# Six orders of the matmuls in the block pairs of two feed-forwards

## Chip, cores and metric

The kernel runs on one core of one Trainium2 chip. The metric is the device time of one execution in microseconds (us); for several executions the median is taken. One core has TensorE (matmuls), VectorE (DVE in the rows), ScalarE (ACT), GpSimd (POOL) and SyncE (SP), each with its own instruction queue, and 16 DMA engines that all queues share. Matmuls write into PSUM, which has eight banks; all else lies in SBUF.

## What is computed

One layer of a streaming encoder for 512 new frames of one stream and 64 of another, together 576 columns, with 1024 features on the rows. Cut to what matters here:

```python
x = x + 0.5 * swiglu_ffn(rms_norm(x, ffn1_norm), ffn1_w_gate_up, ffn1_w_down)   # 1024 -> 2 x 2816 -> 1024
...                                                   # mixer: products by w_in, two convolutions,
...                                                   # w_a_out, w_b_out, w_out
x = x + 0.5 * swiglu_ffn(rms_norm(x, ffn2_norm), ffn2_w_gate_up, ffn2_w_down)

def swiglu_ffn(x, w_gate_up, w_down):
    gate, up = jnp.split(x @ w_gate_up, 2, axis=-1)
    return (jax.nn.silu(gate) * up) @ w_down
```

All values are fp32. The hidden width is 2816, that is 22 tiles of 128, numbered i = 0 to 21.

## The kernel before

**Products in three parts.** Each fp32 operand is split into a high part that TensorE takes in one pass and a low part, the rest. A product is then three matmuls for each 128 x 128 piece of weights: high weights by high activations, high by low, low by high. The stationary operand is always a 128 x 128 piece of weights, the moving one half of the frames, 288 columns. In a plain product (`mm`, lines 431 to 442) both halves of the frames are done piece by piece into two banks, in the order of `SIX`: four matmuls on the high weights, alternating between the halves, then two on the low ones.

**Block pairs.** For most tiles i the gate and the up projection are not made by four plain products but by seven block products on sums and differences (a scheme of seven products for a 2 x 2 block matrix). `pair(i, hs, last)` (lines 863 to 907) does one tile: for n = 0 to 6 it fetches unit n of the weights with `ws.get`, calls `block` with that unit and operand list `bs[n]`, and runs `steps[n - 1]`, which reads finished banks with ScalarE or VectorE. Of the moving operands, n = 0, 2, 3 and 4 are the first half of their tiles, n = 1, 5 and 6 the second. `block` (lines 452 to 459) takes one bank and writes its twelve matmuls k by k (four pieces of 128 rows), each time high-high, high-low, low-high. Feed-forward 1 has 18 such pairs (i = 4 to 21), feed-forward 2 has 21 (i = 1 to 21), in four groups of 5, 5, 6 and 6 tiles; after each group come the products by `w_down` for it. Pairs are 39 x 84 = 3276 of the 9718 matmul instructions.

**Weights.** `Stream` (lines 202 to 318) loads raw weights by SyncE's queue, and makes from each a unit: ScalarE casts the high part; the low part is made by VectorE (`how` "dve"), or ScalarE writes minus the high part and a DMA of GpSimd's queue adds the raw weights to it ("dma"). In a pair units 0, 4 and 6 are "dma", the others "dve". `ws.get(n)` begins units up to six ahead, so where it stands in the program sets where these casts and subtractions stand in the queues of ScalarE and VectorE. Each engine works its queue in program order. Units live in turn in four tiles `u` (high and low part in one tile) and in tiles `g` (one for each part).

**Left over from a pair.** The last steps of a pair (the second half of up, the hidden product, its split) go into `rest`, and the next pair pops one after each block. In feed-forward 2 tile 0 is a plain one whose gate, hidden product and split also wait in `rest` for pair 1.

**Sums over partitions** (`Sum.total`, lines 592 to 614) are four matmuls with a matrix of ones, `ones_r`, between products.

Of the kernel before, what the change touches and what calls it, by code (L numbers as in the profile page):

```python
# [22 lines left out]
KU = KT // 2  # L23
T = SEQ + DSEQ
H = T // 2
# [86 lines left out]
def tile_encoder_step(  # L112
# [51 lines left out]
    def bank():  # L164

        if not spare:
            t = psum2()
            spare.extend((t[:, 0, :], t[:, 1, :]))
        return spare.pop(0)
# [279 lines left out]
            got += [(w, kk) for kk in range(ws.units[n][1])]  # L449
        return got  # L450

    def block(w, xs):

        q = bank()[:, :H]
        for k in range(KU):
            (whi, wlo), (xh, xl) = w, xs[k]
            for m, (l, r) in enumerate(((whi, xh), (whi, xl), (wlo, xh))):
                pe.matmul(q, l[:, k, :], r, start=k == m == 0, stop=k == KU - 1 and m == 2)
        return q


# [358 lines left out]
    def ffn(f, xg, sums, finish, forms, R=None, todo=()):  # L820
        todo = list(todo)

        rest = []


        def plain(i, hs):
            nonlocal R
            t, up = ttile(), (f, "u", i)
            ps = product((f, "g", i), xg, order=IN_TURN if f == "f2" and i == 0 else None)
            got = None if up in early else chunks(up)  # L830
            if R is None:
                R = rstd(sums)
            ups = product(up, xg, got=got)
            hs.append(None)
            at = len(hs) - 1

            def gate():
                dve.tensor_tensor(halves(t), ps, halves(R), op=ALU.mult)
                sca.activation(t, t, AF.Silu)

            def hidden():
                dve.tensor_tensor(halves(t), ups, halves(t), op=ALU.mult)
                hs[at] = high(t)

            def parts():
                hs[at] = hs[at], low(t, hs[at])

            if f == "f2":
                rest.extend((gate, hidden, parts))
                return  # L850
            gate()
            forming()
            hidden()
            forming()
            parts()
            forming()

        def forming():
            if todo:
                for step, p in todo.pop(0):  # L860
                    step(p)

        def pair(i, hs, last):
            qu, uu, t, cu = (ttile() for _ in range(4))
            q1, u2, u3, u4 = half(qu, 0), half(qu, 1), half(uu, 0), half(uu, 1)
            q = []

            def q7():
                dve.tensor_tensor(u3, q[3], u2, op=ALU.add)
                dve.tensor_tensor(half(cu, 1), u3, q[2], op=ALU.subtract)  # L870

            def gate():
                dve.tensor_tensor(half(t, 1), q[5], u4, op=ALU.add)
                dve.tensor_tensor(t, t, R, op=ALU.mult)
                sca.activation(t, t, AF.Silu)

            steps = (
                lambda: sca.copy(q1, q[0]),
                lambda: dve.tensor_tensor(u2, q[1], q1, op=ALU.subtract),
                lambda: dve.tensor_tensor(u4, q[2], u2, op=ALU.subtract),  # L880
                q7,
                lambda: dve.tensor_tensor(half(t, 0), q[4], q1, op=ALU.add),
                gate,
            )
            for n, xs in enumerate(bs):
                q.append(block(ws.get(plan[f, "s", i][n]), xs))
                if n > 0:
                    steps[n - 1]()
                if rest:
                    rest.pop(0)()  # L890

            hs.append(None)
            at = len(hs) - 1

            def up():
                if last:
                    dve.tensor_tensor(t, t, R, op=ALU.mult)
                dve.tensor_tensor(half(cu, 0), q[6], u3, op=ALU.add)

            def hidden():  # L900
                dve.tensor_tensor(cu, cu, t, op=ALU.mult)
                hs[at] = high(cu)

            def parts():
                hs[at] = hs[at], low(cu, hs[at])

            rest.extend((up, hidden, parts))

        for g, grp in enumerate(GROUPS):
            hs = []  # L910
            for i in grp:
                if i < PLAIN[f]:
                    plain(i, hs)
                    continue
                if i == PLAIN[f]:
                    ws.ahead = AHEAD_UNITS
                    bs = forms.operands(xg)
                pair(i, hs, grp[-1] == FT - 1)
            while rest:
                rest.pop(0)()  # L920
            spare.clear()
            if grp[-1] < FT - 1:
                for j, ps in enumerate(both([(f, "d", g, j) for j in range(2)], hs, turn=True)):
                    update(j, ps, R)
                for j in range(2, KT):
                    update(j, product((f, "d", g, j), hs), R)
            else:
                finish(g, hs)
# [509 lines left out]
```

## Time and profile before

| what | value |
|---|---|
| median of three runs | 1294.17 us (1290.7 to 1296.05) |
| span of the profiled execution, first to last instruction | 1290.1 us |
| TensorE busy | 1279.4 us, 99% |
| VectorE, ScalarE, GpSimd busy | 925.1, 765.5, 361.6 us |
| mean granted TensorE clock | 0.997 of full speed |

The profile is of one execution; its own time outside the trace is not given apart from the three runs, so its span stands beside their median. A row of the timeline begins with the start in us from the span's beginning and a length in us, then engine, line, operation, the tiles out<-in, the shapes and how many equal instructions in a row (x12) it stands for. Nearly every instruction is issued through one helper, line 88, so the tile names tell them apart. Lengths of matmuls overlap, since they are pipelined: the pace is read from the starts of successive rows, divided by the count.

### The profile page before, as it was taken

The numbers are of one execution on the slowest core, as the hardware profiler recorded it, in microseconds if no ns is written. First come the engines' busy times: TensorE is split into PE (matmuls) and PEld (weight loads), VectorE is DVE, ScalarE is ACT, GpSimd is POOL, SyncE is SP. The second block draws the span as 40 slices with busy tenths as digits, with TensorE's granted clock in tenths as the row PEclk, the third lists the DMA queues.
The fourth block names the chain that finished last, engine by engine and source line by source line (L and its number), as shares of the span: only waits on it lengthen the run. The fifth ranks groups of instructions, "written<-read, shape, count | busy, mean of one in ns | idle before, by whom it ended". The sixth has DMA issues, their size and how long they took to land.

```text
span 1290.1 us, 25702 instructions
## 1 busy us (share of the span) xinstructions
PE 1279.4 (99%) x9728; PEld 1277.5 (99%) x9728; DVE 925.1 (72%) x1539; ACT 765.5 (59%) x1359; POOL 361.6 (28%) x460
## 2 busy tenths in 40 slices
PE   9999999999999999999999999999999999999997
PEld 9999999999999999999999999999999999999997
DVE  6868668748846998888895166656867848847956
ACT  7655646646776645555444576477665655654664
POOL 0032332232333444333321221122142141241230
PEclk9999999999999999999999999999999999999998
DMA  7286787886799898788885767696687696796783
GB/s 220 70 181 154 163 180 155 177 181 149 154 224 232 174 200 173 165 172 174 172 172 124 163 142 154 151 236 145 139 175 171 151 197 151 164 204 138 158 172 97
DMA packets 286812, 215.26 MB, mean 167 GB/s; under 512 B 15456, under 2 KB 248928, under 8 KB 286688
## 3 DMA queue, kind: packets, MB, share of 16 engines
q0 software_dynamic: 56160, 92.43, 43.3%
q1 hardware_dynamic: 228784, 120.35, 32.8%
q8 instruction: 77, 1.26, 0.4%
q10 hardware_dynamic: 1744, 0.83, 0.2%
q14 instruction: 47, 0.39, 0.1%
HBM read 116.17 MB, written 4.98 MB: 94 GB/s over the span
## 4 chain that ended last, share of the span: by engine, by line
PE 92%; issue 4%; DVE 2%; DMA 1%; ACT 1%; POOL 0%; DVEq 0%; POOLq 0%; ACTq 0%
PE mm L88 92%; DVE tmp L88 0%; DMA g<-raw 0%; DMA raw<-in_w_b_out_dram 0%; DVE x L88 0%; DVE g L88 0%; DMA u<-raw 0%; ACT act L88 0%; DVE w L88 0%; POOL u L88 0%; DVE act L88 0%; ACT u L88 0%; ACT w L88 0%; ACT g L88 0%; POOL g L88 0%
## 5 line engine op out<-in xcount | busy, mean ns | idle before, releaser
L88 PE MATMUL mm<-act,u 128*128 128x288 f32 x4758 | 668.3, 293 | 0.1
L88 PEld LDWEIGHTS mm<-act,u 128*128 128x128 f32 x4758 | 638.9, 188 | 0.4 <-DMA u<-raw 0.3
L88 PE MATMUL mm<-act,g 128*128 128x288 f32 x3030 | 432.9, 294 | 0.9 <-DMA g<-raw 0.9
L88 PEld LDWEIGHTS mm<-act,g 128*128 128x128 f32 x3030 | 410.3, 188 | 1.1 <-DMA g<-raw 1.1
L88 POOL DMA_DIRECT2D u<-raw x197 | 172.3, 874 | 481.7 <-ACT u L88 317.4
L88 PE MATMUL mm<-act,act 128*128 128x288 f32 (+2 forms) x1896 | 259.9, 293 | 0.0
L88 PEld LDWEIGHTS mm<-act,act 128*128 128x128 f32 x1896 | 252.2, 188 | 0.5 <-ACT act L88 0.3
L88 ACT CAST u<-raw 128x512 fp32r<-128x512 f32 (+2 forms) x207 | 118.8, 574 | 172.0 <-PE mm L88 136.7
L88 POOL DMA_DIRECT2D g<-raw x126 | 109.9, 872 | 297.4 <-ACT g L88 242.7
L88 DVE SCALAR_TENSOR_TENSOR w<-g,prm,w 128x606 f32<-128x606 f32 x232 | 179.3, 844 | 1.4 <-ACT w L88 1.4
L88 DVE TENSOR_TENSOR tmp<-mm,tmp 128x288 f32<-128x288 f32 (+1 forms) x251 | 112.9, 459 | 70.3 <-PE mm L88 53.7
L88 ACT ACTIVATE u<-u 128x512 fp32r<-128x512 f32 (+2 forms) x197 | 116.8, 593 | 6.2
L88 ACT CAST g<-raw 128x512 fp32r<-128x512 f32 (+2 forms) x136 | 75.1, 553 | 43.9 <-DMA raw<-in_ffn_w_down_dram 17.6
L88 DVE SCALAR_TENSOR_TENSOR tmp<-mm,r 128x576 f32<-128x576 f32 x48 | 36.3, 757 | 76.6 <-PE mm L88 76.6
L88 POOL DMA_DIRECT2D act<-raw x67 | 59.1, 883 | 108.3 <-ACT act L88 94.5
L88 ACT CAST act<-tmp 128x576 fp32r<-128x576 f32 x92 | 61.9, 675 | 43.1 <-DVE tmp L88 42.1
L88 ACT CAST g<-w 128x512 fp32r<-128x512 f32 x79 | 49.0, 620 | 64.4 <-DVE w L88 58.6
L88 ACT CAST u<-w 128x512 fp32r<-128x512 f32 x81 | 50.2, 619 | 61.0 <-DVE w L88 43.6
L88 DVE TENSOR_TENSOR act<-tmp,act 128x576 fp32r<-128x576 f32 x92 | 67.5, 754 | 18.1 <-ACT act L88 16.5
L88 ACT ACTIVATE g<-g 128x512 fp32r<-128x512 f32 (+2 forms) x126 | 72.1, 572 | 4.0
L88 DVE TENSOR_TENSOR w<-raw,raw 128x512 f32<-128x512 f32 x82 | 56.2, 685 | 16.2 <-DMA raw<-in_ffn_w_gate_up_dram 11.2
L88 ACT ACTIVATE tmp<-tmp 128x576 f32<-128x576 f32 x47 | 32.2, 686 | 45.1 <-DVE tmp L88 45.0
(86 smaller groups left out, 830.6 us busy)
## 6 DMA issues: line engine op xcount, KB each, us to landing
raw<-in_ffn_w_gate_up_dram SPq DMA_DIRECT2D x171, 256.0 KB, 3.5
u<-raw POOLq DMA_DIRECT2D x140, 256.0 KB, 4.2
raw<-in_w_in_dram SPq DMA_DIRECT2D x112, 256.0 KB, 3.8
raw<-in_ffn_w_down_dram SPq DMA_DIRECT2D x96, 192.0 KB, 3.8
g<-raw POOLq DMA_DIRECT2D x69, 256.0 KB, 4.2
act<-raw POOLq DMA_DIRECT2D x61, 256.0 KB, 4.4
g<-raw POOLq DMA_DIRECT2D x43, 192.0 KB, 4.5
u<-raw POOLq DMA_DIRECT2D x41, 192.0 KB, 4.5
```

Of the source, the lines that this page charges most:

```text
L88: return self.tc.keep_in_program_order(fn(*args, **kwargs))
```

## The change

`block` gets a parameter v that picks one of six orders for the three kinds of matmul (HH high-high, HL high weights by low activations, LH low weights by high activations); `blocks` writes them and sets start and stop by the first and last matmul of each product. The pair of tile i uses v = i mod 6. Order 0 is that of before. Order 2 does two pieces' high matmuls and then their two low ones, order 3 swaps HH and HL, order 4 does all high matmuls and then the four low ones, order 5 begins each piece with LH. With v = 1, blocks 0 and 1, 2 and 3, 4 and 5 are written side by side into two banks, by `TURNS`; both units are fetched, and both blocks issued, before the step that followed the first one. Block 6 of such a pair has order 0. The mixer's two block pairs call `block` without v.

```diff
-    def block(w, xs):
-
-        q = bank()[:, :H]
-        for k in range(KU):
-            (whi, wlo), (xh, xl) = w, xs[k]
-            for m, (l, r) in enumerate(((whi, xh), (whi, xl), (wlo, xh))):
-                pe.matmul(q, l[:, k, :], r, start=k == m == 0, stop=k == KU - 1 and m == 2)
+    HH, HL, LH = range(3)
+
+    BLOCK_ORDERS = (
+        [(k, m) for k in range(KU) for m in (HH, HL, LH)],
+        None,
+        [(k + d, m) for k in (0, 2) for d, m in (
+            (0, HH), (0, HL), (1, HH), (1, HL), (0, LH), (1, LH))],
+        [(k, m) for k in range(KU) for m in (HL, HH, LH)],
+        [(k, m) for k in range(KU) for m in (HH, HL)] + [(k, LH) for k in range(KU)],
+        [(k, m) for k in range(KU) for m in (LH, HH, HL)],
+    )
+
+    def blocks(parts, orders):
+
+        qs = [bank()[:, :H] for _ in parts]
+        for n, (i, k, m) in enumerate(orders):
+            (whi, wlo), xs = parts[i]
+            xh, xl = xs[k]
+            l, r = ((whi, xh), (whi, xl), (wlo, xh))[m]
+            mine = [o for o in orders if o[0] == i]
+            pe.matmul(
+                qs[i], l[:, k, :], r, start=(i, k, m) == mine[0], stop=(i, k, m) == mine[-1]
+            )
+        return qs
+
+    TURNS = [
+        (i, k, m) for k in range(KU)
+        for i, m in ((0, HH), (0, HL), (1, HH), (1, HL), (0, LH), (1, LH))
+    ]
+
+    def block(w, xs, v=0):
+
+        q, = blocks([(w, xs)], [(0, k, m) for k, m in BLOCK_ORDERS[v]])
         return q
...
+            v = i % len(BLOCK_ORDERS)
             for n, xs in enumerate(bs):
-                q.append(block(ws.get(plan[f, "s", i][n]), xs))
+                if v == 1 and n < 6:
+                    if n % 2 == 0:
+                        two = [(ws.get(plan[f, "s", i][n + d]), bs[n + d]) for d in range(2)]
+                        q.extend(blocks(two, TURNS))
+                else:
+                    q.append(block(ws.get(plan[f, "s", i][n]), xs, 0 if v == 1 else v))
                 if n > 0:
                     steps[n - 1]()
```

**TensorE, pair 1 of feed-forward 2, before**, from the middle of block 0 into block 1. The names are the PSUM tile, the moving tile, and the stationary one: `g_11152` and `g_11153` are the high and low part of unit 0, `u_11181` holds both parts of unit 1.

```order
6030 L88 MATMUL mm_11390<-act_10968,g_11152 128x288
6031 L88 MATMUL mm_11390<-act_10969,g_11152 128x288
6032 L88 MATMUL mm_11390<-act_10968,g_11153 128x288
6033 L88 MATMUL mm_11390<-act_11128,g_11152 128x288
6034 L88 MATMUL mm_11390<-act_11129,g_11152 128x288
6035 L88 MATMUL mm_11390<-act_11128,g_11153 128x288
6036 L88 MATMUL mm_11390<-act_10827,u_11181 128x288
6037 L88 MATMUL mm_11390<-act_10985,u_11181 128x288
```

Unit 1 is read for the first time after all twelve matmuls of block 0. The same pair after, from its first matmul:

```order
5928 L88 MATMUL mm_11396<-act_10732,g_11152 128x288
5929 L88 MATMUL mm_11396<-act_10733,g_11152 128x288
5930 L88 MATMUL mm_11396<-act_10827,u_11181 128x288
5931 L88 MATMUL mm_11396<-act_10985,u_11181 128x288
5932 L88 MATMUL mm_11396<-act_10732,g_11153 128x288
5933 L88 MATMUL mm_11396<-act_10827,u_11181 128x288
5934 L88 MATMUL mm_11396<-act_10814,g_11152 128x288
```

Unit 1 is read from the third matmul on, and the low part of unit 0 by the fifth instead of the third.

**ScalarE at the same place, before.** `r_11313` is the root of the norm, `tmp_11241` the silu of tile 0, `u_11407` unit 0 of pair 2 (cast, then minus the high part for the DMA), `tmp_11372` the copy of the first bank of pair 1.

```order
936 L88 ACTIVATE r_11313<-mm_11314 128x576
937 L88 CAST g_11379<-raw_10941 128x512
938 L88 ACTIVATE g_11380<-g_11379 128x512
939 L88 ACT_TABLE_LOAD
940 L88 ACTIVATE tmp_11241<-tmp_11241 128x576
941 L88 CAST u_11407<-raw_11246 128x512
942 L88 ACTIVATE u_11407<-u_11407 128x512
943 L88 COPY tmp_11372<-mm_11390 128x288
```

The unit of pair 2 stands behind the silu. After (the unit is `u_11392` now):

```order
936 L88 ACTIVATE r_11313<-mm_11314 128x576
937 L88 CAST g_11379<-raw_10941 128x512
938 L88 ACTIVATE g_11380<-g_11379 128x512
939 L88 CAST u_11392<-raw_11246 128x512
940 L88 ACTIVATE u_11392<-u_11392 128x512
941 L88 ACT_TABLE_LOAD
942 L88 ACTIVATE tmp_11241<-tmp_11241 128x576
943 L88 COPY tmp_11372<-mm_11396 128x288
```

It stands ahead of the silu and its table load now.

**VectorE at the same place, before.** `tmp_11241` is gate and then hidden product of tile 0, `act_11444` the low part of the hidden product, `w_...` sums of weights, `g_11428` the low part of unit 1 of pair 2, `tmp_11372<-mm_11390` a step of pair 1 on its banks.

```order
1058 L88 TENSOR_TENSOR w_11377<-raw_11069,raw_11101 128x512
1059 L88 TENSOR_TENSOR tmp_11241<-mm_11242,r_11313 128x576
1060 L88 TENSOR_TENSOR w_11405<-w_11377,raw_11246 128x512
1061 L88 TENSOR_TENSOR tmp_11241<-mm_11323,tmp_11241 128x576
1062 L88 TENSOR_TENSOR tmp_11372<-mm_11390,tmp_11372 128x288
1063 L88 TENSOR_TENSOR act_11444<-tmp_11241,act_11425 128x576
1064 L88 TENSOR_TENSOR g_11428<-w_11405,g_11427 128x512
1065 L88 TENSOR_TENSOR w_11447<-raw_11246,raw_11069 128x512
```

The step on the banks and the split stand ahead of the weights. After:

```order
1058 L88 TENSOR_TENSOR w_11377<-raw_11069,raw_11101 128x512
1059 L88 TENSOR_TENSOR w_11390<-w_11377,raw_11246 128x512
1060 L88 TENSOR_TENSOR tmp_11241<-mm_11242,r_11313 128x576
1061 L88 TENSOR_TENSOR tmp_11241<-mm_11323,tmp_11241 128x576
1062 L88 TENSOR_TENSOR g_11428<-w_11390,g_11427 128x512
1063 L88 TENSOR_TENSOR w_11431<-raw_11246,raw_11069 128x512
1064 L88 TENSOR_TENSOR tmp_11372<-mm_11396,tmp_11372 128x288
1065 L88 TENSOR_TENSOR act_11463<-tmp_11241,act_11425 128x576
```

One sum of weights moved ahead of the gate, and the low part of unit 1 with the next sum moved ahead of the step and the split.

## Rows read from the trace of the kernel before

**Rows 1.** The page: busy time by engine; the chain by engine.

```profile
PE 1279.4 (99%) x9728; PEld 1277.5 (99%) x9728; DVE 925.1 (72%) x1539; ACT 765.5 (59%) x1359; POOL 361.6 (28%) x460
...
PE 92%; issue 4%; DVE 2%; DMA 1%; ACT 1%; POOL 0%; DVEq 0%; POOLq 0%; ACTq 0%
```

**Rows 2.** Waits of TensorE's weight loads, three of six: us, times, longest.

```profile
PEld mm L88 <- DMA g<-raw: 1.1, 1, 1.1
...
PEld mm L88 <- DMA u<-raw: 0.3, 1, 0.3
PEld mm L88 <- DVE act L88: 0.2, 1, 0.2
```

**Rows 3.** TensorE's timeline, feed-forward 1, second group: pair 5 from end to end.

```profile
99.55 1.74 PE L88 MATMUL mm<-act,u 128*128 128x288 f32 x12
...
110.59 1.08 PE L88 MATMUL mm<-act,g 128*128 128x288 f32 x7
```

**Rows 4.** The same, third group: pair 11 from end to end.

```profile
197.13 1.75 PE L88 MATMUL mm<-act,u 128*128 128x288 f32 x12
...
208.23 1.49 PE L88 MATMUL mm<-act,g 128*128 128x288 f32 x10
```

**Rows 5.** The same, products of the mixer around one sum over partitions.

```profile
682.42 3.28 PE L88 MATMUL mm<-act,act 128*128 128x288 f32 x24
685.54 3.29 PE L88 MATMUL mm<-act,u 128*128 128x288 f32 x24
688.67 0.69 PE L88 MATMUL mm<-tmp,ones_r 128*128 128x288 f32 x4
689.20 3.32 PE L88 MATMUL mm<-act,act 128*128 128x288 f32 x24
692.36 3.32 PE L88 MATMUL mm<-act,u 128*128 128x288 f32 x24
```

**Rows 6.** Windows of the mixer between sums: us, then busy us and count by engine.

```profile
402.00:688.00 286.00, 286.00 (x2202) 286.00 (x2201) 249.30 (x381) 150.60 (x246) 104.64 (x157) 1.00 0.83 176
...
716.00:808.00 92.00, 92.00 (x710) 92.00 (x709) 46.30 (x76) 55.57 (x90) 20.58 (x24) 1.00 0.73 157
```

**Rows 7.** TensorE's timeline, feed-forward 2, pair 2: first and last block.

```profile
919.24 1.90 PE L88 MATMUL mm<-act,u 128*128 128x288 f32 x12
920.98 1.75 PE L88 MATMUL mm<-act,g 128*128 128x288 f32 x12
...
928.91 2.08 PE L88 MATMUL mm<-act,u 128*128 128x288 f32 x12
930.83 0.42 PE L88 MATMUL mm<-act,g 128*128 128x288 f32 x2
```

**Rows 8.** ScalarE's timeline, pairs 1 and 2 of feed-forward 2.

```profile
909.62 0.63 ACT L88 ACTIVATE g<-g 128x512 fp32r<-128x512 f32 x1
...
913.42 0.69 ACT L88 ACTIVATE tmp<-tmp 128x576 f32<-128x576 f32 x1 [1.88 <-DVE tmp L88]
...
922.72 0.69 ACT L88 ACTIVATE tmp<-tmp 128x576 f32<-128x576 f32 x1 [0.85 <-DVE tmp L88]
923.31 0.60 ACT L88 CAST u<-raw 128x512 fp32r<-128x512 f32 x1
```

**Rows 9.** VectorE's timeline, pair 1 of feed-forward 2.

```profile
912.64 0.75 DVE L88 TENSOR_TENSOR tmp<-mm,r 128x576 f32<-128x576 f32 x1
913.31 0.68 DVE L88 TENSOR_TENSOR w<-w,raw 128x512 f32<-128x512 f32 x1
...
915.60 0.46 DVE L88 TENSOR_TENSOR tmp<-mm,tmp 128x288 f32<-128x288 f32 x1 [0.70 <-ACT tmp L88]
916.17 0.76 DVE L88 TENSOR_TENSOR act<-tmp,act 128x576 fp32r<-128x576 f32 x1
916.85 0.69 DVE L88 TENSOR_TENSOR g<-w,g 128x512 fp32r<-128x512 f32 x1
```

**Rows 10.** GpSimd's timeline: the DMA of the last unit of pair 2.

```profile
925.55 0.86 POOL L88 DMA_DIRECT2D u<-raw  x1 [4.36 <-ACT g L88]
```

## Prediction

> **What bounds the kernel now.** I read the page from the top: TensorE is busy for 99% of a span of 1290.1 us, in 9728 matmuls with as many weight loads, and the chain of work that ended last is 92% TensorE [rows 1]. The list of waits says how little of that is waiting for weights: in the whole execution it names two that a weight's DMA ended, of 1.1 and 0.3 us, the first in the products by w_out, which the change leaves alone, and one of 0.2 us for weights that VectorE makes (tile act: none of a pair of the feed-forwards) [rows 2]. So time can move in two ways only: by the pace at which matmuls follow each other, or by new stops.
>
> For the pace I took the starts of equal runs from TensorE's timeline. A pair of the second group of the first feed-forward goes from 99.55 to 110.59 us: 11.04 us for 84 matmuls, 131.4 ns each [rows 3]. A pair of the third group takes 208.23 - 197.13 = 11.10 us, 132.1 ns each [rows 4]. A product of the mixer, whose matmuls stand in another order (four on one stationary operand, alternating between two halves of the frames and two banks, then two on the low part), puts 24 matmuls in 3.12 us, 130.0 ns; after a four-matmul sum over partitions the same code needs 3.16 us, 131.7 ns [rows 5], and after the next such sum it is back, 710 matmuls in 92.0 us [rows 6]. The reader is to see three things there. The orders of before, blocks and products, lie within 130.0 and 132.1 ns, 1.6%. One and the same order has two paces, and changes between them where the alternation is broken. And 131.7 ns comes both from products that keep one stationary operand for four matmuls and, between 131.4 and 132.1, from blocks that keep it for two.
>
> **The change part by part.**
>
> *Counts.* Nothing is added: both programs have the same matmuls, each with its own load, the same DMAs and the same work on VectorE and ScalarE. Cost 0.
>
> *Orders 2 to 5 inside a block* (26 of the 39 pairs; six more keep order 0). A block still has twelve matmuls, into one bank, all on one half of the frames; high times high and high times low stay neighbours on the same stationary operand, so each block still has eight changes of it. What moves is where the low part is read. By the paces above I take 0 for it. Bounds: if all 26 pairs ran at the best pace seen, 130.0 ns, 26 x 84 x about 1.7 ns = 3.7 us less; orders 3 and 5 put two matmuls with the same moving operand side by side (28 times in each of 13 pairs, 364 in all), which no row of before shows; between the paces seen, 2.1 ns apart, that is at most 0.8 us either way.
>
> *Order 1, two products side by side* (seven pairs: 7, 13, 19 of the first feed-forward, 1, 7, 13, 19 of the second; six of seven blocks each, 504 matmuls). They now alternate between two banks, and in two of the three turns between the two halves, as a mixer product does. Its nearest rows are those products, 130.0 or 131.7 ns, against 131.4 to 132.1 for the blocks: between 504 x 2.1 = 1.1 us less and 504 x 0.3 = 0.2 us more. I take 0.
>
> *When weights are needed.* The second block of a turn now starts two matmuls after the first, not twelve, so units 1, 3 and 5 are wanted ten matmuls, 1.3 us, earlier. Those three are made by VectorE, six units ahead; the list names no wait for such a unit of a pair [rows 2]. Covered, cost 0; if the cover were gone, up to 1.3 us a turn. Orders 2 and 4 want the first low part two and six matmuls later: free. Order 5 wants it two, 0.26 us, earlier; its six pairs show no wait now [rows 2]: 0, at most 6 x 0.26 = 1.6 us.
>
> *The one place with no cover* is the start of the second feed-forward. Pair 2 (from 919.24 us) loses 0.16 us in its first block (919.24 to 920.98, against 1.58 us for a block) and 0.34 in its last (928.91 to 930.83) [rows 7], both waiting for a low part that comes by DMA. Pair 1 is now a side-by-side one, and this is where its calls in a new sequence tell.
> First, the copy of unit 0 of pair 2 stood on ScalarE behind a silu that started at 913.42 [rows 8]; now it stands ahead of it, and can run at 910.3, when ScalarE is through with what stands before it (909.62 + 0.63) [rows 8]. Its DMA comes 3 us earlier, and the 0.16 us goes.
> Second, VectorE loses time in pair 1. One sum of weights (0.60 us) moves ahead of the gate at 912.64, so silu and the hidden product follow 0.6 us later. Then the low part at 916.85, which needs a cast on ScalarE behind that hidden product, moves ahead of two steps that had filled its wait at 915.60 and 916.17 [rows 9]; they and all after them come later by what they last, 0.57 + 0.68 us, less the little by which the low part is earlier: about 1.1 us. The gate of pair 1 and the silu at 922.72 then slip to about 923.8, and with them the cast of the last unit behind it (923.31) [rows 8] and its DMA (925.55) [rows 10], which landed as TensorE went on, and now lands near 930.4. TensorE, 0.16 us earlier and needing the low part only at the fifth matmul (928.75 + 4 x 0.132 = 929.3), waits some 1.1 us. Net 1.1 - 0.5 = **+0.6 us**. Bounds: -0.5 if VectorE catches up, +1.7 if the lag is double.
>
> *Banks.* A turn takes both banks at its start. There are eight, and a bank is used again eight blocks later (12.6 us); cost 0.
>
> **Sum.** 0 + 0 + 0 + 0.6 = +0.6 us: the profiled execution would go from 1290.1 to 1290.7 us of span. The three runs have a median of 1294.17, so 4.1 us lie around the span or between executions; on the median that is **1294.8 us**.
>
> **A rule that speaks for more.** The rows show a spacing of 130.0 to 132.1 ns for 288 columns, which is 10 to 12 ns above the 120 ns that 288 columns take at 2.4 GHz, in every order tried so far. The Trainium skill (TensorE: Matmul & The Clock Gate, "Back-to-back issue gap") gives N/2.4 + 2.5 ns for a warm matmul that no load holds up, an estimate of 122.5 ns here; an order that reached it would save 33 x 84 x 9 ns = 25 us and end near 1269. No row here supports it: four uses of one operand in a row pace like two.
>
> **The rivals.**
> *An order that runs better.* If some new order stays at the best pace of the trace, and all changed pairs do, 22 pairs at 11.04 and 17 at 11.10 us come to 10.92: 2.6 + 3.1 = 5.7 us less, about 1289. For it: the two paces exist. Against: every block of before goes through eight moving tiles and eight stationary operands, and its pace does not care.
> *The pace of the mixer flips.* The pace is kept through hundreds of matmuls and changes where four matmuls break the alternation [rows 5, 6]. The side-by-side pairs are a new alternation; the first feed-forward has three, an odd number. If each flips it, the mixer runs at 131.7 where it ran at 130.0: 2202 + 710 matmuls x 1.67 ns [rows 6], less the 192 of the four products between two sums that would go the other way, +4.5 us, about 1299.3. Against: the pairs of before alternate too, between blocks, and keep the pace.
> *Slower: the lag of VectorE costs at every side-by-side pair.* If the 1.1 us of lag reaches the last unit of the following pair at all seven places, as it does at the one above, it costs 7 x 1.1 - 0.5 = 7.2 us, 1301.4. It decides where that unit's DMA lands less than 1.1 us ahead of its use. Against: the other places show no wait now, and VectorE, 72% busy, can catch up.
> That the program does otherwise than said is out: the instruction order shows each order in its place.
>
> **How the numbers follow.** Forecast 0.68; flipped pace 0.18; lag everywhere 0.08; better order 0.06. A difference under about 0.5% (6.5 us) is what a measurement of this kernel cannot tell from none. Faster by more needs a pace that no row shows: 0.04. Slower by more: the lag, and a flip with some of the lag: 0.10. Within: 0.86. The runs of before spread from 1290.7 to 1296.05, so a median of the same kernel may fall 2 or 3 us off. Range: down to 1290.5 (half of the better-order case and the spread), up to 1299.6 (the flipped pace), 8 in 10.
>
> **What would show it.** In the timeline of the changed kernel, blocks of orders 2 to 5 take 1.57 to 1.59 us; a turn of two takes 3.12 to 3.18; the mixer's products keep 3.12 us for 24 matmuls (3.16 would be the flip). In pair 2 of the second feed-forward the first block has no stop and the last has one of about 1.1 us; TensorE's list of waits has no other new entry in the feed-forwards. I am wrong if an order's blocks stand outside 1.56 to 1.60 us without a wait: then neighbourhood of operands does set the pace.

## The result, and the profile after

| what | before | after |
|---|---|---|
| median of 17 executions each | 1294.1 us (1290.65 to 1296.05) | 1297.25 us (1292.53 to 1298.68) |
| ratio, 95% interval | | 1.0027 [1.0017, 1.0037] |
| span of the profiled execution | 1290.1 us | 1295.3 us |

The change costs 3.2 us by the medians and 5.2 us between the profiled executions. The difference of these two numbers is part of the result: the executions of before gather at two levels, eight from 1290.65 to 1291.34 us and nine from 1294.1 to 1296.05; 15 of the 17 of after lie between 1296.1 and 1298.7. Why there are two levels, and to which the profiled execution of before belongs, comes out below.

The page of after, busy time by engine, as the first line of [rows 1]:

```profile
PE 1283.8 (99%) x9728; PEld 1282.1 (99%) x9728; DVE 926.0 (71%) x1539; ACT 764.9 (59%) x1359; POOL 360.7 (28%) x460
```

TensorE has the same 9728 matmuls, and 4.4 us more busy time; no other engine changed by more than 1 us. So it is pace, and the stages tell where. Starts of the same matmul in both traces:

| start of | before | after | lost so far |
|---|---|---|---|
| pair 7 of feed-forward 1 | 121.64 | 121.49 | -0.15 |
| mixer's first product | 401.62 | 401.36 | -0.26 |
| mixer, end of the second stretch of [rows 6] | 808.61 | 812.91 | 4.30 |
| pair 1 of feed-forward 2 | 908.15 | 912.50 | 4.35 |
| pair 2 | 919.24 | 923.55 | 4.31 |
| pair 3 | 930.83 | 935.67 | 4.84 |
| third product by w_down of the last group | 1251.43 | 1256.70 | 5.27 |

4.56 us are lost between 401 and 813 us, in the mixer, whose instructions the change leaves alone. Feed-forward 2 adds 0.9 us (4.35 to 5.27), 0.53 of it in pair 2. TensorE's timeline around the same sum over partitions as [rows 5]:

```profile
688.92 3.33 PE L88 MATMUL mm<-act,u 128*128 128x288 f32 x24
692.08 0.69 PE L88 MATMUL mm<-tmp,ones_r 128*128 128x288 f32 x4
692.61 3.28 PE L88 MATMUL mm<-act,act 128*128 128x288 f32 x24
695.73 0.55 PE L88 MATMUL mm<-act,u 128*128 128x288 f32 x3
```

It is [rows 5] turned round: 3.16 us for 24 matmuls ahead of the sum (131.7 ns each) and 3.12 us behind it (130.0 ns). Before it was 3.12 ahead and 3.16 behind. The long stretches are the slow ones now. TensorE alone in a window inside the first (columns: window, its length in us, busy us and count of PE, granted clock, DMA share, GB/s), after:

```profile
402.00:687.00 285.00, 285.00 (x2167) 1.00 0.83 175
```

and before:

```profile
402.00:687.00 285.00, 285.00 (x2195) 1.00 0.83 176
```

28 matmuls fewer in 285 us, at the same granted clock of 1.00, the same DMA share of 0.83, and 175 against 176 GB/s. So neither the clock nor the load on the DMA engines tells the two apart.

The pace of the pairs, in the timeline of after: the first matmuls of pairs 6, 7, 8 and 9 of feed-forward 1.

```profile
110.45 1.74 PE L88 MATMUL mm<-act,g 128*128 128x288 f32 x12
...
121.49 0.43 PE L88 MATMUL mm<-act,u 128*128 128x288 f32 x2
...
132.55 1.75 PE L88 MATMUL mm<-act,g 128*128 128x288 f32 x12
...
143.65 1.75 PE L88 MATMUL mm<-act,u 128*128 128x288 f32 x12
```

Pair 6 (order 0) takes 11.04 us, as in [rows 3]. Pair 7, side by side, takes 11.06. Pair 8 (order 2) takes 11.10: the pace of [rows 4], in a group where before had 11.05 to the end. It goes on to pair 9; in the next group 10 to 12 take 11.05, and 14 and 15, behind the side-by-side pair 13, 11.10 again.

The start of feed-forward 2, in answer to [rows 7, 8, 10]. TensorE, first block of pair 2 and its last:

```profile
923.55 1.75 PE L88 MATMUL mm<-act,u 128*128 128x288 f32 x12
925.13 1.75 PE L88 MATMUL mm<-act,g 128*128 128x288 f32 x12
...
933.06 0.69 PE L88 MATMUL mm<-act,u 128*128 128x288 f32 x4
934.51 1.32 PE L88 MATMUL mm<-act,u 128*128 128x288 f32 x8 [0.76 <-DMA u<-raw]
935.67 1.83 PE L88 MATMUL mm<-act,g 128*128 128x288 f32 x12
```

ScalarE's silu of pair 1, and GpSimd's DMA of the last unit of pair 2:

```profile
928.13 0.68 ACT L88 ACTIVATE tmp<-tmp 128x576 f32<-128x576 f32 x1 [1.42 <-DVE tmp L88]
```

```profile
930.95 0.86 POOL L88 DMA_DIRECT2D u<-raw  x1 [5.39 <-ACT g L88]
```

The first block has no stop (1.58 us). The silu comes 928.13 - 923.55 = 4.58 us after the start of pair 2, before 3.48; the DMA is issued 18.45 us after the start of pair 1, before 17.40; the last block takes 2.61 us, 1.03 more than a block, where before lost 0.34. Pair 2 takes 12.12 us against 11.59.

### The profile page after: what moved, and what is told of

The parts are those of the page before. It is cut to its first block, busy times and chain, and to the rows that moved or that the text cites. A ratio compares the mean times of both kernels' runs of the same rounds, so it can differ in the third digit from the quotient of the medians.

```text
span 1295.3 us, 25678 instructions
## 1 busy us (share of the span) xinstructions
PE 1283.8 (99%) x9728; PEld 1282.1 (99%) x9728; DVE 926.0 (71%) x1539; ACT 764.9 (59%) x1359; POOL 360.7 (28%) x460
## 4 chain that ended last, share of the span: by engine, by line
PE 95%; issue 2%; DVE 1%; DMA 1%; ACT 0%; POOL 0%; DVEq 0%; POOLq 0%; ACTq 0%
PE mm L88 95%; DMA g<-raw 0%; DMA raw<-in_w_b_out_dram 0%; DVE tmp L88 0%; DVE g L88 0%; DVE x L88 0%; DMA u<-raw 0%; DMA gains<-in_params_dram 0%; ACT act L88 0%; DVE w L88 0%; POOL u L88 0%; DVE act L88 0%; POOL g L88 0%; DVE u L88 0%; DVEq L1460 0%
## 5 line engine op out<-in xcount | busy, mean ns | idle before, releaser
L88 PE MATMUL mm<-act,u 128*128 128x288 f32 x4758 | 691.8, 294 | 0.8 <-DMA u<-raw 0.8
L88 PEld LDWEIGHTS mm<-act,u 128*128 128x128 f32 x4758 | 649.5, 188 | 1.0 <-DMA u<-raw 1.0
L88 PE MATMUL mm<-act,g 128*128 128x288 f32 x3030 | 454.3, 294 | 0.9 <-DMA g<-raw 0.9
L88 PEld LDWEIGHTS mm<-act,g 128*128 128x128 f32 x3030 | 418.7, 188 | 1.2 <-DMA g<-raw 1.1
```

What stands on the lines that cost most here:

```text
L88: return self.tc.keep_in_program_order(fn(*args, **kwargs))
```

## The experiments

Four questions were open: which part of the change costs; whether each side-by-side pair flips the pace (the rival of the prediction, by which an even number of pairs would change nothing) or sets it; which of the three turns does it; and why before has two levels.

**Orders 2 to 5 alone.**

```diff
-            v = i % len(BLOCK_ORDERS)
+            v = (0, 0, 2, 3, 4, 5)[i % 6]
```

> The changed kernel with order 0 in place of the side-by-side order 1; orders 2 to 5 stay. Theory (the side-by-side pairs switch the pace): pairs take 11.05 or 11.10 us exactly as before, the mixer's products 3.12 us for 24 matmuls, the late low parts at pair 2 of feed-forward 2 cost 0.1 to 0.3 us instead of 0.5; ratio to before 0.999 to 1.000. Rival (any new order inside a block disturbs the pace): the mixer stays at 3.16 us for 24, ratio about 1.003.

Measured: ratio 1.001 [0.9995, 1.0024], median 1293.34 us, at the two levels of before. Window of the mixer:

```profile
402.00:687.00 285.00, 285.00 (x2194) 1.00 0.84 176
```

As before. In its profile every pair from 5 to 21 of feed-forward 1 lies within 0.001 us of before, whatever its order. Orders 2 to 5 are neutral. Its pair 2 of feed-forward 2, though, lost 1.27 us in its last block where 0.1 to 0.3 was expected, and so stopped for longer than that of after, with ScalarE's and VectorE's queues as before:

```profile
927.02 0.69 PE L88 MATMUL mm<-act,u 128*128 128x288 f32 x4
928.71 1.32 PE L88 MATMUL mm<-act,u 128*128 128x288 f32 x8 [1.00 <-DMA u<-raw]
929.87 1.74 PE L88 MATMUL mm<-act,g 128*128 128x288 f32 x12
```

```profile
923.82 0.86 POOL L88 DMA_DIRECT2D u<-raw  x1 [4.36 <-PE mm L88]
```

The DMA was issued 17.40 us after the start of pair 1, exactly as before, but the matmul that waited for it started only 4.89 us later; in after that was 3.56 us. The size of this stop hangs on a landing time that differs by over a microsecond from one execution to the next.

**Side by side alone.**

```diff
-            v = i % len(BLOCK_ORDERS)
+            v = int(i % 6 == 1)
```

> The kernel before with the side-by-side order alone, in the same seven pairs; all others keep order 0. Theory: all of the loss is here: mixer at 3.16 us for 24 matmuls, about +4.5 us, and a stop of 1 us or a little more at the last block of pair 2 of feed-forward 2 (its low part is wanted two matmuls earlier than in the changed kernel), +0.6 to +0.9; span +5 to +5.5 us, ratio 1.003 to 1.004. Rival: ratio about 1.000.

Measured: ratio 1.003 [1.0014, 1.0045], median 1296.01 us, span 1294.0. The mixer has the 2167 matmuls of after in the window; pairs 8 and 9 take 11.10 us. From 401 us on it loses what after loses: 4.56 us in the mixer and 1.0 in the pairs and products of feed-forward 2. So the whole loss is here. The span is 3.9 us above that of before and not the expected 5 to 5.5, since stretches that the change does not touch took less: 0.9 us up to pair 4, 0.5 between the mixer and feed-forward 2.

**Two side-by-side pairs, 16 and 19 of feed-forward 1**, an even number in one group:

```diff
-            v = i % len(BLOCK_ORDERS)
+            v = int(f == "f1" and i in (16, 19))
```

> The kernel before with two side-by-side pairs only, 16 and 19 of feed-forward 1, both in the last group ahead of the mixer. Theory as predicted (each such pair flips the pace): two flips cancel, pairs 17 and 18 take 11.10 us, 20 and 21 take 11.05, the mixer stays at 3.12 us for 24 matmuls, span as before within 0.5 us. Rival (such a pair sets one pace, whatever it was): 17, 18, 20 and 21 all take 11.10 us and the mixer 3.16, span +4.5 us.

Measured: 1296.0 us, span 1294.2. First blocks of pairs 17 and 18, of pair 21, and the products behind it:

```profile
301.53 1.75 PE L88 MATMUL mm<-act,u 128*128 128x288 f32 x12
...
312.63 1.75 PE L88 MATMUL mm<-act,g 128*128 128x288 f32 x12
...
345.87 1.75 PE L88 MATMUL mm<-act,u 128*128 128x288 f32 x12
...
356.97 3.21 PE L88 MATMUL mm<-act,g 128*128 128x288 f32 x23
```

Pair 17 takes 11.10 us and pair 21 too; pair 19 itself took 11.05. The second pair did not undo the first, and the mixer is slow (2167 in the window). A side-by-side pair sets the pace; it does not flip it.

**The pace turned once more ahead of the mixer.** `both` makes two products piece by piece, and with `turn` it crosses them once: at the second piece come four matmuls of the first product, all six of the second, then the last two of the first. Here is after with that in the last products of feed-forward 1:

```diff
-        ps = both([("f1", "d", g, j) for j in range(2)], hs)
+        ps = both([("f1", "d", g, j) for j in range(2)], hs, turn=True)
```

> The changed kernel with one more thing: the first two down products after the last group of feed-forward 1 are written in the order with a turn at their second piece, as those of the other groups are. If the loss is the mixer's pace, carried over from side-by-side pair 19, the turn switches it back: the mixer at 3.12 us for 24 matmuls, 4.5 us less than the changed kernel less 0.4 for the down products, so +0.5 to +1 us on before, ratio 1.000 to 1.001. Rival (the mixer is slow for another reason, later weights or contention): ratio stays at 1.003.

Measured: ratio 1.0001 [0.9989, 1.0013], median 1292.53 us (1291.82 to 1294.39). The products around the sum:

```profile
684.82 3.29 PE L88 MATMUL mm<-act,u 128*128 128x288 f32 x24
687.95 0.69 PE L88 MATMUL mm<-tmp,ones_r 128*128 128x288 f32 x4
688.48 3.32 PE L88 MATMUL mm<-act,act 128*128 128x288 f32 x24
691.64 0.55 PE L88 MATMUL mm<-act,u 128*128 128x288 f32 x3
```

3.13 us ahead of the sum, 3.16 behind, as before. All side-by-side pairs are still there; one crossing 40 us ahead of the mixer takes the loss away. So the loss is a pace that the mixer takes over from what ran ahead of it, and the order of a few matmuls sets that pace.

**Single turns, in places of their own.**

```diff
-            v = i % len(BLOCK_ORDERS)
+            turns = {
+                ("f1", 5): (0,), ("f1", 7): (2,), ("f1", 8): (4,),
+                ("f1", 10): (0,), ("f1", 12): (4,), ("f1", 14): (2,),
...
+            }.get((f, i), ())
...
-                if v == 1 and n < 6:
+                if n - n % 2 in turns:
```

> The kernel before with a single turn side by side in some pairs, all else in order 0: blocks 0 and 1 in pairs 5, 10 and 19 of feed-forward 1 and 14 and 17 of feed-forward 2; blocks 2 and 3 (both on the first half) in 7 and 14 of the first, 6 of the second; blocks 4 and 5 in 8, 12 and 17 of the first, 8, 12 and 19 of the second. Theory (the alternation of halves sets the pace, and which half it ends in before the next run): the pair after a turn of 0 and 1 takes 11.05 us whatever it was before, the pair after a turn of 4 and 5 takes 11.10, the pair after a turn of 2 and 3 is as the one before it. Rival (two banks in turn are enough): the turns of 2 and 3 change it too.

Measured, first blocks of pairs 7, 8, 9 and the products behind (turn of blocks 2 and 3 in pair 7, of 4 and 5 in pair 8):

```profile
120.66 1.74 PE L88 MATMUL mm<-act,u 128*128 128x288 f32 x12
...
131.71 1.74 PE L88 MATMUL mm<-act,g 128*128 128x288 f32 x12
...
142.75 1.75 PE L88 MATMUL mm<-act,u 128*128 128x288 f32 x12
...
153.85 4.92 PE L88 MATMUL mm<-act,g 128*128 128x288 f32 x36
```

Pair 7 11.05, pair 8 11.04, pair 9 11.10. Below, pairs of 11.05 us are called fast and those of 11.10 slow. All fourteen turns agree. Blocks 2 and 3 are both of the first half: nothing changes (three times), so two banks in turn are not enough. After a turn of blocks 0 and 1 the following pairs take 11.05 (five times, three of them behind slow pairs), after one of 4 and 5 they take 11.10 (six times, each behind fast pairs); in both kinds of turn the two blocks are on different halves. A side-by-side pair ends with 4 and 5, and leaves 11.10.

**The pace chosen.** Turns of 0 and 1 in the first pairs of groups, 4 and 5 in their last, since slow pairs leave 130.0 ns to the products behind them; no crossing in the products by w_down and w_out.

```diff
+                ("f1", 9): (4,), ("f1", 10): (0,), ("f1", 15): (4,), ("f1", 5): (0,), ("f1", 16): (0,),
...
-                for j, ps in enumerate(both([(f, "d", g, j) for j in range(2)], hs, turn=True)):
+                for j, ps in enumerate(both([(f, "d", g, j) for j in range(2)], hs)):
...
```

> Uses the switch: blocks 0 and 1 side by side in the first pair of a group, blocks 4 and 5 in its last where down products follow (not in the last group of feed-forward 1), no turn in the first two down products and the first two products by w_out. Theory: pairs 11.05 us in all groups but the first, down products 30 matmuls in 3.90 us in place of 3.95, products by w_out at 3.12 for 24, mixer as before; 3 us less than before, ratio 0.997 to 0.998. Rival (the pace does not follow these switches, or the turns were hiding a late operand): ratio 1.000 or above.

Measured: ratio 0.9975 [0.9961, 0.999], median 1289.33 us, span 1287.7. Pairs 5 to 21 of feed-forward 1 take 11.04 to 11.05 us, and the products by w_down behind groups 2 and 3 run at 130.2 ns. The products by w_out, expected at 3.12 us for 24, stay at 3.16. Its median is below those of both kernels, with as many matmuls.

**Sums that alternate.** In before the four matmuls of a sum take the first half of the frames twice, then the second twice. Here they take first, second, first, second (this is what "ordered by half" means in the expectations). A product does not alternate in that strict way: by `SIX`, the six matmuls of a piece take first, first, second, second, first, second. So a sum of before repeats the first four of such a six; and `TURNS` gives two blocks on different halves the same six, put in among blocks that stay on one half for twelve matmuls.

```diff
-            for s, (i, e) in enumerate(spans):
-                for n, (one, v) in enumerate(terms):
+            for n, (one, v) in enumerate(terms):
+                for s, (i, e) in enumerate(spans):
```

> The kernel before with the four matmuls of each sum over partitions ordered high first half, high second half, low first half, low second half, in place of both of a half together. Theory (the sequence of halves switches the pace): without two and two in the sum the pace is not switched there: the mixer keeps the 3.16 us for 24 matmuls of the down products ahead of it, span some 3 to 5 us more than before. Rival (a sum switches because ScalarE or another operand comes between): mixer at 3.12 as before.

Measured: 1289.56 us, span 1287.7. Around the same sum:

```profile
684.42 3.29 PE L88 MATMUL mm<-act,u 128*128 128x288 f32 x24
687.54 0.70 PE L88 MATMUL mm<-tmp,ones_r 128*128 128x288 f32 x4
688.08 3.29 PE L88 MATMUL mm<-act,act 128*128 128x288 f32 x24
691.21 3.28 PE L88 MATMUL mm<-act,u 128*128 128x288 f32 x24
```

3.12 to 3.13 us on both sides: a sum written so does not change the pace. The expectation had the slow pace carried through; this execution came to the mixer with 130.0 ns, and carried that. A sum like this that keeps the slow pace is in the trace of the last kernel below.

**The queues alone.** Before, with the units of pair 1 of feed-forward 2 fetched two by two, and every block in order 0:

```diff
+                if early_two and n < 6:
+                    if n % 2 == 0:
+                        two = [ws.get(plan[f, "s", i][n + d]) for d in range(2)]
+                        q.extend(block(two[d], bs[n + d]) for d in range(2))
```

> The kernel before with one edit in pair 1 of feed-forward 2: the two units of each of three couples of blocks are fetched together and both blocks issued before the step between them, but the twelve matmuls of a block stay in order 0, one block after the other. Theory (the later DMA at pair 2 comes from the queues of ScalarE and VectorE): the DMA of the last unit of pair 2 is issued 18.4 to 18.5 us after pair 1 starts, as in the changed kernel, not 17.4 as before; no stop in the first block of pair 2, one of 0.8 to 1.6 us in the last; the pace of all pairs as before. Rival (the order of the matmuls delays it): 17.4 us.

Measured: 1291.63 us. The DMA of pair 2's last unit, and pair 2's first block and last:

```profile
925.63 0.86 POOL L88 DMA_DIRECT2D u<-raw  x1 [5.39 <-ACT g L88]
```

```profile
918.26 1.75 PE L88 MATMUL mm<-act,u 128*128 128x288 f32 x12
919.85 1.75 PE L88 MATMUL mm<-act,g 128*128 128x288 f32 x12
...
927.78 0.43 PE L88 MATMUL mm<-act,u 128*128 128x288 f32 x2
929.36 1.58 PE L88 MATMUL mm<-act,u 128*128 128x288 f32 x10 [1.16 <-DMA u<-raw]
930.78 1.49 PE L88 MATMUL mm<-act,g 128*128 128x288 f32 x10
```

Issued 18.46 us after the start of pair 1 (907.17), as in after; no stop in the first block, 1.42 us in the last. The sequence of calls is enough for both, without any new order on TensorE. The pace of the pairs did not stay as before, though, as was expected: behind this longer stop, pairs 5 to 9 take 11.09 to 11.10 us, where before had 11.05.

**One turn only: blocks 0 and 1, or 4 and 5, of pair 16 of feed-forward 1**, in before. The second kernel has (4,) in place of (0,) and is otherwise the same.

```diff
+            turns = {("f1", 16): (0,)}.get((f, i), ())
```

> The kernel before with one turn, blocks 0 and 1 of pair 16 of the first feed-forward. Theory that the executions of before lie round two levels, 1290.2 to 1291.7 and 1294 to 1296 us, because its early part leaves either pace by chance and nothing up to the mixer overrides it: here pairs 17 to 21 take 11.05 us and the mixer 130.0 ns (24 products in 3.12 us) in every execution, so all but one or two of the executions lie between 1290 and 1292.5 us, median 1291.2. Rival that the two levels come from something else (the DMAs of the start, the second feed-forward): executions at both levels as before, about half above 1294.

> The kernel before with one turn, blocks 4 and 5 of pair 16 of the first feed-forward; only which blocks are side by side differs from the kernel with the turn of blocks 0 and 1. Theory that the turn sets the pace for what follows: pairs 17 to 21 at 11.10 us, the mixer at 131.67 ns (24 in 3.16 us), all but one or two of the executions between 1293.5 and 1296.5 us, median 1295.0, ratio between the two kernels about 1.003. Rival that the changed kernel loses by the seven side-by-side pairs themselves (their banks, units or steps): one turn costs nothing, executions spread as before.

Measured beside 23 executions of before (1290.5 to 1296.53; 11 of them below 1293, 12 above): with 0 and 1 all twelve executions lie from 1289.86 to 1292.43, median 1291.17, ratio 0.9981 [0.9969, 0.9993]. With 4 and 5 six lie from 1290.0 to 1292.0 and six from 1294.6 to 1295.4, ratio 0.9994 [0.998, 1.0008]. Windows of the mixer, with 0 and 1:

```profile
402.00:687.00 285.00, 285.00 (x2194) 1.00 0.84 175
```

and with 4 and 5 (an execution of 1294.77 us):

```profile
402.00:687.00 285.00, 285.00 (x2166) 1.00 0.82 174
```

The first expectation holds: one turn, 110 us ahead of the mixer, removes the upper level. So the two levels of before are the two paces of the mixer. No execution of before at its upper level was traced, so this is inferred; the sizes agree with it. From its first product to the end of its second long stretch the mixer takes 406.99 us in the profile of before and 411.55 in that of 1294.77 us. From pair 4 to the mixer, before takes 344.79 us; the kernel whose sums alternate, which came to its pairs with the other pace, takes 344.05. 4.56 less 0.74 is 3.8 us; the medians of the two groups of before, 1291.14 and 1294.76, lie 3.6 apart. The early part of before leaves one or the other: pair 4 takes 11.09 us in the profile of before and 11.05 in that of the kernel with one turn of 0 and 1, although the program is the same up to there. The second expectation missed: if 4 and 5 always set one pace, all twelve should be slow.

**Turns of 4 and 5 in a row**, in pairs 17 to 20, to tell whether such a turn flips after all:

```diff
+                ("f1", 16): (0,), ("f1", 17): (4,), ("f1", 18): (4,), ("f1", 19): (4,),
+                ("f1", 20): (4,),
```

> The kernel before with single turns: in the first feed-forward blocks 0 and 1 in pairs 11, 12 and 16, blocks 2 and 3 in pair 13, blocks 4 and 5 in pair 14 and in four pairs in a row, 17 to 20; in the second, blocks 0 and 1 in pair 16, 4 and 5 in pairs 17 and 18, 2 and 3 in pair 19. Theory that a turn of blocks 4 and 5 changes the pace to the other one, whichever it was, while a turn of blocks 0 and 1 always leaves the faster pace of pairs: pairs 12 and 13 at 11.05, pair 15 at 11.10; pair 17 at 11.05, pair 18 in between (four or five blocks at the slow pace, near 11.08), pair 19 at 11.05, pair 20 near 11.08, pair 21 at 11.05; in the second, pair 18 near 11.08, pairs 19 to 21 at 11.05. Then the two levels of the kernel with one turn of blocks 4 and 5 follow from the pace with which it is entered. Rival that a turn of blocks 4 and 5 always leaves the slower pace of pairs: pairs 18 to 21 all at 11.10, and pairs 18 to 21 of the second feed-forward too; then something behind pair 16 makes the two levels.

Measured: 1292.6 us, span 1290.5. Pairs 17 to 21 take 11.05, 11.07, 11.08, 11.08 and 11.10 us; the pairs with a turn are shorter only by the blocks of the turn itself, and each next one begins at the slow pace. In feed-forward 2 pairs 18 to 21 take 11.07, 11.10, 11.10, 11.10. So it doesn't flip the pace of pairs, and the theory of this expectation falls too. But behind pair 21 stands something that neither side expected. Rows of the products by w_down, and one product of the mixer with the sum behind it:

```profile
361.43 4.90 PE L88 MATMUL mm<-act,u 128*128 128x288 f32 x36
366.17 2.54 PE L88 MATMUL mm<-act,g 128*128 128x288 f32 x18
...
685.38 3.29 PE L88 MATMUL mm<-act,u 128*128 128x288 f32 x24
688.50 0.69 PE L88 MATMUL mm<-tmp,ones_r 128*128 128x288 f32 x4
```

and the same place with one turn of 4 and 5:

```profile
361.12 4.84 PE L88 MATMUL mm<-act,u 128*128 128x288 f32 x36
365.80 2.50 PE L88 MATMUL mm<-act,g 128*128 128x288 f32 x18
```

After pairs of the same 11.10 us the products run at 366.17 - 361.43 = 4.74 us for 36 (131.7 ns) in the one and 365.80 - 361.12 = 4.68 (130.0 ns) in the other, and the mixer, behind one more sum, at 130.0 in the first (688.50 - 685.38 = 3.12) and 131.7 in the second. The slow pairs have two kinds, alike in their time and different in what they leave. A turn of 4 and 5 entered from fast pairs leaves the first kind (products 130.0, mixer slow); entered from slow pairs it leaves the second (products 131.7, mixer at 130.0). That would answer the six and six: pair 16 is entered fast or slow by the chance of the early part. No execution of the kernel with one turn was traced at its lower level, so for that kernel it is argued, not shown.

That there are two kinds does not rest on this one place. In feed-forward 2 of the same trace, pair 17 has a turn of 4 and 5 entered from fast pairs and pair 18 one entered from slow pairs; behind pair 21 (11.10 us), the second product by w_down takes 4.74 us for its 36 matmuls:

```profile
1247.07 4.90 PE L88 MATMUL mm<-act,g 128*128 128x288 f32 x36
1251.81 2.54 PE L88 MATMUL mm<-act,u 128*128 128x288 f32 x18
```

Nine other traces have a pair 21 of 11.10 us there, none of them behind such a turn, and in all nine these 36 take 4.68. A stop can make the second kind too. Before and the kernel with pairs 16 and 19 run the same matmuls from the mixer on, and both take 11.09 us for pair 1 of feed-forward 2; pair 2, with its stops, takes 11.59 and 11.79, pair 4 takes 11.10 in both, and the products by w_down behind it, crossing included, run at 131.8 and 130.3 ns.

In the changed kernel a turn of 0 and 1 stands ahead of each turn of 4 and 5, so that it is always entered fast, and the mixer is slow.

**All together**: the chosen turns, no crossing, sums that alternate.

```diff
+                ("f1", 4): (4,), ("f1", 5): (0,), ("f1", 9): (4,), ("f1", 10): (0,),
+                ("f1", 15): (4,), ("f1", 16): (0,), ("f1", 21): (4,),
...
```

> Single turns of blocks 0 and 1 in the first pair of groups 2 and 3 and of blocks 4 and 5 in the last pair of every group of both feed-forwards, no crossing of the halves in the products by w_down and w_out, and the sums over partitions ordered by half, so that they no longer change the pace. Theory that the order of the halves sets a pace which then persists: pairs 11.04 to 11.05 us in groups 2 and 3, products at 130.0 ns (24 in 3.12 us) in the mixer, in the products between its sums and in those by w_down of groups 1 to 3 of the first feed-forward; span 1286 to 1287.5 us, ratio to before 0.996 to 0.997, executions within 2 us of each other. Rival that the sums or the DMAs around them cost by themselves: no better than the kernel with chosen turns alone, span 1287.7, ratio 0.9975.

Measured: ratio 0.996 [0.9944, 0.9975], median 1288.83 us (1287.99 to 1289.57, six executions), span 1286.5. The last products by w_out, and the first ones of feed-forward 2 behind the sum:

```profile
886.28 3.32 PE L88 MATMUL mm<-act,g 128*128 128x288 f32 x24
889.45 3.32 PE L88 MATMUL mm<-act,u 128*128 128x288 f32 x24
...
898.92 0.69 PE L88 MATMUL mm<-tmp,ones_r 128*128 128x288 f32 x4
899.45 3.33 PE L88 MATMUL mm<-act,g 128*128 128x288 f32 x24
902.62 3.32 PE L88 MATMUL mm<-act,u 128*128 128x288 f32 x24
```

The pairs of the first feed-forward take 11.04 to 11.05 us from 4 to 21, and the mixer keeps 130.0 to 130.1 ns in both stretches of [rows 6] and between them. The products by w_out are still slow, 3.17 us for 24, and here the alternating sum carries the slow pace through: 3.17 us behind it as well. With the sum of before at this place the kernel with the chosen pace goes from 3.16 to 3.12. So an alternating sum changes neither pace, and one in the order of before changes it. This is the fastest kernel here, by the medians 8.4 us below the changed one, with as many matmuls.

## Why the prediction was right, and where not

1297.25 us lies in the range, 2.5 above the value, and the difference is below 0.5%, as forecast. The likeliest case is not what happened, though; the rival on the pace is. That the value came so near is luck: 4.5 us of the mixer are missing from the sum, and the step from span to time, which is some 2 us too large, hides half of it.

- **Orders inside a block, 0.** Right: the run with them alone shows it, pair by pair. Two neighbours on the same moving operand (orders 3 and 5), which no row of before showed, cost nothing.
- **Side by side, 0.** This step failed. The seven pairs themselves cost what was said: 11.04 to 11.06 us. What I left out of the term is what they leave behind. I had read that one order has two paces, that a pace is kept through hundreds of matmuls and changes where the alternation is broken, and that these pairs are a new alternation; and put it at 0.18 because the pairs of before alternate between blocks and keep the pace. But a sequence of halves that repeats from pair to pair is no break; a turn put among blocks is. That sentence was the weak one. I also took the products for a plain alternation of halves that a sum breaks; they go first, first, second, second, first, second, and the sum repeats the first four. Its size was right: 4.5 us worked out, 4.56 us found between 401 and 813 us.
- **That it flips, by an odd number of pairs.** Wrong: with two pairs in a group the mixer is slow as well. The answer was right for the wrong reason.
- **Weights wanted earlier, 0; banks, 0; lag at every side-by-side pair.** The first two held and the third did not come: outside pair 2 no pair of feed-forward 2 takes over 11.18 us, and none of pairs 5 to 21 of feed-forward 1 over 11.10.
- **The place without cover, +0.6.** The steps came as said: the stop in the first block goes, the silu comes 1.10 us later (1.1 said), the DMA's issue 1.05 later, the last block stops for 1.03 us (1.1 said), pair 2 takes 0.54 us more. The run with the queues alone shows the same without side-by-side blocks. That the size fits so well is luck. The stops vary: with the queues as before, pair 2 takes 11.36 to 12.65 us in the ten traces and loses under 0.1 us in its first block in four of them; with the new sequence of calls it takes 12.13 to 12.52 in four, without a stop in the first block. One profile doesn't tell that.
- **From span to time, 4.1 us.** Mis-sized. I took the distance between the span and the median for work around the span. The runs show 1.7 to 2.3 us (1297.25 against 1295.3, 1289.57 against 1287.6). So the profiled execution of before took about 1290.1 + 1.9 = 1292 us, with its mixer at 130.0 ns like the lower level; the other 2 us came from the two levels mixed in a median. With 1292 in place of 1294.17, 5.2 us more is 1297.2, which is what was measured. The three times given at the start, 1290.7, 1294.17 and 1296.05, already held them, and I read them as spread.
- **A better order, 1289.** Not this change, but 1288.83 is there for the taking with the two paces chosen. The rule of the Trainium skill (TensorE: Matmul & The Clock Gate, "Back-to-back issue gap"), an estimate of 122.5 ns, is given there for an isolated matmul, and the section says that in a stream of weight loads and matmuls both set the spacing. None of these kernels met it: the lowest pace held through a stage at 288 columns, each matmul with its load, is 130.0 ns, and the measurement decides.

Open: why the pace depends on the order of the halves at all; whether the half of the operand or the PSUM bank that changes with it does it, since two banks alone do nothing (blocks 2 and 3) but no run tests the half without the bank; what in the early part chooses the pace; and the two executions of after at 1292.5 and 1293.1 us, of which there is no profile.

## What to carry to other kernels

Where a kernel's executions gather at two levels, look for one stage that runs at two paces with the same instructions, clock and DMA load, and compare its matmul counts in equal windows; a median over such executions is a mixture, and one profile shows only one of them. A change of order inside one stage can cost nothing there and set the pace of another stage 100 us later, so compare the traces by the starts of stages and not by the lines that were edited. Where TensorE is busy for 99%, a pace of 1.3% can be worth more than all stops (here 4.6 us in the mixer, against 3.9 us in the list of waits of TensorE's weight loads before), and it can be chosen by the order of the operands.

## What was not expected of the hardware

Matmuls of 288 columns with a weight load each, at a granted clock of 1.00, follow each other at 130.0 or 131.7 ns in one and the same code, through 2200 of them, depending on how the two halves of the moving operand followed each other long before. Two blocks side by side on different halves, four matmuls of a sum in the order first, first, second, second, one crossing of two products, and stops can change which; two blocks side by side on the same half, and a sum in the order first, second, first, second, do not. The two paces are two rhythms and not one delay: in pair 6 of before (11.05 us) the starts come in a cycle of four, about 133, 134, 133 and 127 ns apart, in pair 12 (11.10 us) in a cycle of three, about 131, 130 and 135. And pairs that take the same 11.10 us can leave either pace to the products behind them, so that the pace of a stage doesn't tell all of what is carried on.
